# Experts of a mixture layer: the tokens of two pairs gathered at once in float32r halves, 22 weight tiles in flight, and a passage in four pieces

## The chip, the core and the metric

The kernel runs on one core of a Trainium2 chip. The metric is device time in microseconds (us) of one execution; the median of three runs stands for the kernel. Engines are named as in the profile: PE (TensorE, matrix products), DVE (VectorE), ACT (ScalarE), POOL (GpSimd) and SP (SyncE, which here issues the weight transfers).

## What is computed

Two transformer blocks over 256 tokens of width 1024, in float32. Block one is a retention branch and a convolution branch, merged, and then a mixture of 32 experts. Block two is a gated mixer and a dilated attention. The change lies in the experts and in the passage from the first block to the second:

```
def _hier_moe(u, p):
    ...
    top_w, top_i = lax.top_k(jax.nn.softmax(in_grp, axis=-1), EXPERT_TOP_K)   # 2 experts of a group
    ...
    for e in range(N_EXPERTS):                                                # 32 experts, 512 wide
        h = jax.nn.silu(t @ p['w_exp_gate'][e]) * (t @ p['w_exp_up'][e])
        y = y + combine[:, e:e + 1] * (h @ p['w_exp_down'][e])
...
h_lat = _layernorm(ALPHA * h_lat + gt_f * moe, p['ln2_g'], p['ln2_b'])
```

Every token goes to two experts; the reference runs all tokens through all experts with weights that are zero elsewhere. The kernel gathers up to 64 tokens for each expert and leaves the rest to a second pass behind a branch, which these inputs don't enter.

## The kernel before

**Experts.** Two experts form a pair, and a loop runs over 16 pairs. An object of the class `Pair` carries a pair through its steps. `gather` (L928) multiplies the normed tokens hn, 256 x 1024, by a selection matrix gt of 0 and 1 (256 tokens by 2 x 64 places) and so brings the tokens of the two experts to columns, eight chunks of 128x128 with two products each, float32; ACT (L932) and DVE (L934) take them out of PSUM by turns, with scale and shift, to xg. `products` (L945) makes gate and up in two halves, the 64 tokens of an expert as stationary columns, two experts side by side. `act` (L964, L965) makes silu(gate) * up, `turn` (L970) transposes it, ACT copies the result to hT (L972), `down` (L984) multiplies it by the second weight. `combine` (L991 to L999) splits the result of the pair before into two float32r halves and sends the rows back to their tokens by products with gT; `weights` (L956 to L960) prepares the gate weights. The order in the loop is written by hand with `after(...)`, which holds an instruction behind a named other one: the first half of the next pair's gather stands behind the up products, the second behind `turn`.

**Weights.** A pair takes 12 tiles of 128x2048, 1 MB each: gate, up, gate, up and down, two tiles for each of the halves. `moe_tiles` asks for them in order and `fetch` (L124) issues them on SP; each transfer stands behind the one before it on that queue. They go to slots in turn: five of the pool `ring`, some of the pools `ring3` (RING3), `x` (NX) and of the tag x8 (NX8), and further free spaces, 23 in rotation and one for the first tile. A slot is written anew when PE has done with its tile. With SP in order, one late slot holds all later transfers.

**Passage.** With the last `combine` done, DVE makes statistics (L1076, L1117), POOL raises the variance to the power -1/2 (L162; there is a branch ahead of it, which reads `cnti`: L1088), and DVE norms the two row blocks in one instruction each (L1123, 128x1024). PE transposes chunks of the normed rows (L1153), DVE and ACT make scaled features of them (L1161, L1162: ft, xl), and the first products of the mixer follow (L185 to L187). These products run in three parts: `split` makes of a float32 weight the float32r halves h_w (ACT, L179) and l_w (DVE, or POOL where `idle` is set, L181), and PE adds xh*h_w, xl*h_w and xh*l_w. The l_w of the first mixer tile are POOL's, held behind the power: `after(pows[0] if idle else ...)`. After the first quarter of the mixer's columns the residual gets its gain and shift (L1254, L1255), one row block on POOL, one on DVE.

In names of the rows below, `acc` is the memory of the residual rows, `cat` holds the identity for transposes, `mm`, `po`, `tr`, `sc`, `y` are PSUM tiles.

## Time and profile before

| | us |
|---|---|
| median of three runs (1492.33 to 1494.02) | 1493.73 |
| the profiled execution, its own time | 1494.24 |
| its span on the core | 1492.5 |
| PE busy in the span | 1437.1 (96%) |
| DVE busy | 931.9 (62%) |
| ACT busy | 557.2 (37%) |
| POOL busy | 125.1 (8%) |

Times in rows count from the start of the span. Outside the span 1.7 us of the execution lie. PE works nearly all the time over the whole span, so the totals say little; each stage has to be read by itself. The experts run from 500 to 961 us, the passage from there to about 1006 us, the mixer and the attention to the end. In a row of the timeline the first number is the start, the second the time from there to the end of the last instruction in the row, then engine, line, operation, result and operands; in brackets stands how long the engine stood before it and what ended that.

### The profile page before, as it was taken

How to read it: one execution, taken by the hardware profiler on the slowest of the kernel's cores; microseconds unless marked ns; L12 is line 12 of the kernel's file. 1: busy time of each engine (PE TensorE's matmuls, PEld its weight loads, DVE VectorE, ACT ScalarE, POOL GpSimd, SP SyncE). 2: the span in 40 equal slices, each digit the busy share in tenths (PEclk: the TensorE clock that was granted, in tenths of full speed). 3: DMA queues.
4: the chain of work that ended last, by engine and by line, in shares of the span. 5: the costliest groups of instructions: out<-in, count | busy, mean ns of one | idle time of the engine just before them, and what ended most of it. 6: DMA issues, size and time to landing. Idle time of an engine off the chain costs nothing. (4 is left out here: it accounts for less than half of the span.)

```text
span 1492.5 us, 23025 instructions
## 1 busy us (share of the span) xinstructions
PE 1437.1 (96%) x9391; PEld 1098.6 (74%) x9391; DVE 931.9 (62%) x1631; ACT 557.2 (37%) x834; POOL 125.1 (8%) x104
## 2 busy tenths in 40 slices
PE   7999999999999999999999999879999899999997
PEld 4888888888999544444444444369998799999995
DVE  3899998979656533333333333386668566676766
ACT  3855345332564211111111111154444545454543
POOL 0024021200000000000000000030000111101010
PEclk8999999999999999999999999999999999999999
DMA  8863454546777899999999999356554455655530
GB/s 345 339 216 113 155 211 157 197 156 226 288 292 305 317 373 419 420 420 419 420 420 420 420 420 419 151 202 249 183 199 162 149 209 167 209 174 194 184 114 29
DMA packets 60942, 390.37 MB, mean 262 GB/s; under 512 B 7840, under 2 KB 10400, under 8 KB 16800
## 3 DMA queue, kind: packets, MB, share of 16 engines
q1 hardware_dynamic: 55584, 378.37, 64.9%
q10 hardware_dynamic: 5248, 10.49, 2.9%
q8 instruction: 75, 1.23, 0.3%
q14 instruction: 35, 0.29, 0.1%
HBM read 377.29 MB, written 1.05 MB: 253 GB/s over the span
## 5 line engine op out<-in xcount | busy, mean ns | idle before, releaser
L181 DVE TENSOR_TENSOR l_w<-w,h_w 128x1024 fp32r<-128x1024 f32 x228 | 295.7, 1305 | 74.2 <-ACT h_w L179 70.3
L179 ACT CAST h_w<-w 128x1024 fp32r<-128x1024 f32 x232 | 239.4, 1048 | 263.9 <-PE mm L186 145.5
L185 PE MATMUL mm<-xh,h_w 128*128 128x256 f32 x704 | 201.4, 286 | 0.0
L187 PE MATMUL mm<-xh,l_w 128*128 128x256 f32 x704 | 199.4, 283 | 1.4 <-DVE l_w L181 1.4
L186 PE MATMUL mm<-xl,h_w 128*128 128x256 f32 x704 | 199.4, 283 | 0.0
L187 PEld LDWEIGHTS mm<-xh,l_w 128*128 128x128 f32 x704 | 135.3, 192 | 1.6 <-DVE l_w L181 1.6
L185 PEld LDWEIGHTS mm<-xh,h_w 128*128 128x128 f32 x704 | 135.3, 192 | 0.9
L186 PEld LDWEIGHTS mm<-xl,h_w 128*128 128x128 f32 x704 | 135.3, 192 | 0.1
L999 DVE TENSOR_TENSOR acc<-acc,sc 128x512 f32<-128x512 f32 x64 | 41.1, 684 | 135.6 <-PE sc L998 135.6
L185 PE MATMUL mm<-uh,h_w 128*128 128x256 f32 (+1 forms) x400 | 123.4, 309 | 0.8 <-ACT h_w L179 0.8
L187 PE MATMUL mm<-uh,l_w 128*128 128x256 f32 (+1 forms) x400 | 121.4, 304 | 2.7 <-DVE l_w L181 2.7
L945 PE MATMUL gate<-w,xg 128*64 128x512 f32 x512 | 121.9, 596 | 0.5
L186 PE MATMUL mm<-ul,h_w 128*128 128x256 f32 (+1 forms) x400 | 121.0, 303 | 0.0
L945 PE MATMUL up<-w,xg 128*64 128x512 f32 x512 | 120.0, 595 | 0.0
L331 DVE SCALAR_TENSOR_TENSOR cacc<-zp,pka,cacc 128x256 f32<-128x256 f32 x240 | 118.0, 511 | 1.7
L984 PE MATMUL y<-w,hT 128*64 128x512 f32 x512 | 113.9, 596 | 0.7 <-ACT hT L972 0.7
L945 PEld LDWEIGHTS up<-w,xg 128*64 128x64 f32 x512 | 40.4, 137 | 64.9 <-issue 63.9
L945 PEld LDWEIGHTS gate<-w,xg 128*64 128x64 f32 x512 | 40.2, 137 | 64.2 <-issue 62.4
L984 PEld LDWEIGHTS y<-w,hT 128*64 128x64 f32 x512 | 38.8, 136 | 63.8 <-issue 60.5
L187 PE MATMUL mm<-h_w,xl 128*128 128x256 f32 (+1 forms) x256 | 79.9, 313 | 2.7 <-DVE xl L1162 2.7
L187 PEld LDWEIGHTS mm<-uh,l_w 128*128 128x128 f32 x400 | 76.9, 193 | 7.1 <-DVE l_w L181 3.8
L185 PEld LDWEIGHTS mm<-uh,h_w 128*128 128x128 f32 x400 | 77.1, 193 | 6.7 <-ACT h_w L179 1.9
(411 smaller groups left out, 2848.2 us busy)
## 6 DMA issues: line engine op xcount, KB each, us to landing
w<-in_W_dram SPq DMA_DIRECT2D x343, 1024.0 KB, 10.6
sw<-raw ACTq DMA_DIRECT2D x48, 128.0 KB, 4.4
w<-in_W_dram SPq DMA_DIRECT2D x8, 512.0 KB, 11.4
xt<-in_xc_dram SPq DMA_DIRECT2D x4, 512.0 KB, 5.8
sw<-qk ACTq DMA_DIRECT2D x8, 256.0 KB, 4.2
v<-vt ACTq DMA_DIRECT2D x16, 128.0 KB, 2.4
cbt<-in_cb_dram SPq DMA_DIRECT2D x1, 1152.0 KB, 11.3
ya<-in_W_dram SPq DMA_DIRECT2D x2, 512.0 KB, 10.0
```

The lines of the kernel that those rows point to most:

```text
L179: high[:] = [A.copy(h, src)]
L181: low[:] = [(G if idle else V).tensor_tensor(l, src, h.bitcast(F32), op=OP.subtract)]
L185: T.matmul(ps, sh, mh, start=start, stop=False)
L186: T.matmul(ps, sh, ml, start=False, stop=False)
L187: return T.matmul(ps, sl, mh, start=False, stop=stop)
L331: V.scalar_tensor_tensor(cacc[:, m, :], src, pv("dw", m * 31 + t), cacc[:, m, :], op0=OP.mult, op1=OP.add)
L945: done = T.matmul(self.pgu[u][64 * j:64 * j + 64, :], self.xg[:, c, 64 * j:64 * j + 64], self.w[u][j][:, k * 512:(k + 1) * 512], start=c = ...
L984: T.matmul(self.py[n][64 * j:64 * j + 64, :], self.hT[:, c, 64 * j:64 * j + 64], w[j][:, o:o + 512], start=c == 0, stop=c == 3, tile_posit ...
L999: adds.append(V.tensor_tensor(acc[0][:, b, ns], acc[0][:, b, ns], pc, op=OP.add))
```

## The change

Gathers: pairs 0 and 1 are gathered as before. At pair 0 `halve` makes two float32r halves of hn, hh (ACT copies) and hl (DVE subtracts into a float32 tile `rest`, which takes one turn of a weight slot with tag x8, and ACT casts that into hl, which lies in the memory of hn itself). From then on each odd pair up to 13 gathers the two pairs that follow: `Gathering.chunks` makes 32 products of 128x256 (hh and hl, each by the selection of four experts) where two times 32 of 128x128 stood. Even pairs from 2 on don't gather; the second half of `combine` and `weights` moves behind their up products. Slots: NX8 goes from 6 to 5 and RING3 from 3 to 2, so 21 turn and 22 tiles are in flight; tag h gets a fourth buffer. Passage: the norm comes in four pieces of 512 columns, both row blocks of the left half first; POOL's l_w no longer wait for the power, and the other l_w of that stage wait for the last piece; both row blocks of gain and shift go to DVE, behind the last chunk of features. In block two's attention, arguments of `split` shift by one place: POOL now makes the l_w of the second half of the first weight and of the first half of the second, and the casts of the second weight wait for `fed`.

```diff
@@ -29,5 +29,5 @@
 NEG = -1e30
-RING, RING3 = 5, 3
+RING, RING3 = 5, 2
 NX = 3
-NX8 = 6
+NX8 = 5
@@ -179,3 +179,3 @@
             high[:] = [A.copy(h, src)]
-        with after(pows[0] if idle else hold.pop() if hold else la):
+        with after(None if idle else hold.pop() if hold else la):
             low[:] = [(G if idle else V).tensor_tensor(l, src, h.bitcast(F32), op=OP.subtract)]
@@ -903,2 +903,46 @@
+    def affine(dst, ps, m):
+        if m % 2:
+            A.activation(dst, ps, AF.Identity, scale=fA[:, m:m + 1], bias=fB[:, m:m + 1])
+        else:
+            low[:] = [V.tensor_scalar(dst, ps, fA[:, m:m + 1], fB[:, m:m + 1], op0=OP.mult, op1=OP.add)]
+    hnp = []
+    def halve():
+        hh = m2.tile([128, 2, 1024], F32R, name="hh", bufs=1)
+        rest = m1.tile([128, 2, 1024], F32, name="w", tag="x8", bufs=NX8)
+        for b in range(2):
+            A.copy(hh[:, b, :], hn[:, b, :])
+            V.tensor_tensor(rest[:, b, :], hn[:, b, :], hh[:, b, :].bitcast(F32), op=OP.subtract)
+        hl = m1.tile([128, 2, 1024], F32R, name="hl", tag="gb")
+        for b in range(2):
+            A.copy(hl[:, b, :], rest[:, b, :])
+        hnp[:] = [hh, hl]
+    class Gathering:
+        def __init__(self, *pairs):
+            n = 128 * len(pairs)
+            self.gt = m2.tile([128, 2, 256], F32R, name="gt", bufs=1)[:, :, 0:n]
+            self.xg = m2.tile([128, 8, 256], F32, name="xg", bufs=1)[:, :, 0:n]
+            for i, p in enumerate(pairs):
+                p.choose(self.gt, 1, 128 * i)
+                p.xg = self.xg[:, :, 128 * i:128 * i + 128]
+        def chunks(self, m0, name):
+            pg = ps2.tile([128, 2, 256], F32, name=name, bufs=2)[:, :, 0:self.gt.shape[2]]
+            for k in range(2):
+                m = m0 + k
+                for b in range(2):
+                    for i in range(2):
+                        done = T.matmul(pg[:, k, :], hnp[i][:, b, m * 128:(m + 1) * 128], self.gt[:, b, :],
+                                        start=b + i == 0, stop=b + i == 2)
+            for k in range(2):
+                affine(self.xg[:, m0 + k, :], pg[:, k, :], m0 + k)
+            return done
     class Pair:
@@ -906,8 +950,6 @@
-        def __init__(self, load, e0):
-            self.load, self.e0 = load, e0
-            self.gt = m2.tile([128, 2, 128], F32, name="gt", bufs=1)
-            self.choose(self.gt, 1)
+        def __init__(self, load, e0, xg=None):
+            self.load, self.e0, self.xg = load, e0, xg
-        def choose(self, t, k):
+        def choose(self, t, k, o=0):
             for b in range(2):
@@ -915,3 +957,4 @@
                     e = self.e0 + j
-                    low[:] = [V.tensor_scalar(t[:, b, 64 * j:64 * j + 64], iota, prw[:, 0, b, e:e + 1],
+                    at = o + 64 * j
+                    low[:] = [V.tensor_scalar(t[:, b, at:at + 64], iota, prw[:, 0, b, e:e + 1],
                                               prw[:, k, b, e:e + 1], op0=OP.is_equal, op1=OP.mult)]
@@ -919,5 +962,7 @@
         def gather(self, i, cuts=1):
             if i == 0:
-                self.xg = m2.tile([128, 8, 128], F32, name="xg", bufs=1)
-            xg = self.xg
+                self.gt = m2.tile([128, 2, 256], F32, name="gt", bufs=1)[:, :, 0:128]
+                self.choose(self.gt, 1)
+                self.xg = m2.tile([128, 8, 256], F32, name="xg", bufs=1)[:, :, 0:128]
             pg = [ps2.tile([128, 4 // cuts, 128], F32, name="tr", bufs=2) for _ in range(cuts)]
@@ -929,8 +974,3 @@
             for k in range(4):
-                m = 4 * i + k
-                if k % 2:
-                    A.activation(xg[:, m, :], pg[k], AF.Identity, scale=fA[:, m:m + 1], bias=fB[:, m:m + 1])
-                else:
-                    low[:] = [V.tensor_scalar(xg[:, m, :], pg[k], fA[:, m:m + 1], fB[:, m:m + 1], op0=OP.mult,
-                                              op1=OP.add)]
+                affine(self.xg[:, 4 * i + k, :], pg[k], 4 * i + k)
@@ -962,3 +1002,3 @@
         def act(self):
-            self.h = m2.tile([128, 512], F32, name="h", tag="h", bufs=3)
+            self.h = m2.tile([128, 512], F32, name="h", tag="h", bufs=4)
             A.activation(self.h, self.pgu[0], AF.Silu)
@@ -970,3 +1010,3 @@
                 done = T.transpose(ph[:, k, :], self.h[:, k * 128:(k + 1) * 128], ident)
-            self.hT = m2.tile([128, 4, 128], F32, name="hT", tag="h", bufs=3)
+            self.hT = m2.tile([128, 4, 128], F32, name="hT", tag="h", bufs=4)
             A.copy(self.hT, ph)
@@ -991,3 +1031,3 @@
             V.tensor_tensor(py, py, gtf[:, ns], op=OP.mult)
-            yh, yl = (m2.tile([128, 512], F32R, name=k, tag="h", bufs=3) for k in ("ysh", "ysl"))
+            yh, yl = (m2.tile([128, 512], F32R, name=k, tag="h", bufs=4) for k in ("ysh", "ysl"))
             A.activation(yh, py, AF.Copy, scale=self.ws)
@@ -1017,5 +1057,9 @@
-    last_pair, pair = None, Pair(lambda k: tiles[k], 0)
-    for p in range(16):
+    def nth(p):
+        return Pair(lambda k, o=12 * p: tiles[o + k], 2 * p)
+    pairs = [nth(p) for p in range(16)]
+    for p, pair in enumerate(pairs):
         moe_tiles(12 * p + 12)
+        before = pairs[p - 1] if p else None
         if p == 0:
@@ -1034,22 +1078,36 @@
             with after(done):
-                last_pair.combine(0)
+                before.combine(0)
         done = pair.products(1, 0)
-        if last_pair:
+        late_sum = p and p % 2 == 0
+        if p == 0:
+            start()
+        elif not late_sum:
             with after(done):
-                last_pair.combine(1)
+                before.combine(1)
                 pair.weights()
-        else:
-            start()
         done = pair.products(1, 1)
         pair.act()
-        if p < 15:
-            next_pair = Pair(lambda k, o=12 * p + 12: tiles[o + k], 2 * p + 2)
-            with after(done):
-                next_pair.gather(0)
-            done = pair.turn()
-            with after(done):
-                next_pair.gather(1)
-        else:
-            pair.turn()
-        pair.down()
+        with after(done):
+            if p == 0:
+                pairs[1].gather(0)
+                done = pair.turn()
+                pairs[1].gather(1)
+                halve()
+            elif late_sum:
+                before.combine(1)
+                done = pair.turn()
+                pair.weights()
+            elif p < 15:
+                g = Gathering(*pairs[p + 1:p + 3])
+                g.chunks(0, "sc")
+                done = g.chunks(2, "sc")
+                with after(done):
+                    done = pair.turn()
+                with after(done):
+                    g.chunks(4, "tr")
+                    done = g.chunks(6, "sc")
+            else:
+                done = pair.turn()
+        with after(done):
+            pair.down()
         if p == 15:
@@ -1057,3 +1115,2 @@
                 pair.combine(n)
-        last_pair, pair = pair, next_pair
@@ -1097,4 +1154,5 @@
                 pair = Pair(load, 0)
-                for i in range(2):
-                    pair.gather(i)
+                g = Gathering(pair)
+                for m in range(0, 8, 2):
+                    g.chunks(m, "tr")
                 pair.weights()
@@ -1120,5 +1178,6 @@
     bridge(KN["BR"][1], st.rearrange("p a b -> p (a b)"), mv.rearrange("p a b -> p (a b)"), rs)
-    for b in range(2):
-        r = acc[0][:, b, :]
-        V.tensor_scalar(r, r, mv[:, b, 0:1], rs[:, b:b + 1], op0=OP.subtract, op1=OP.mult)
+    for n in range(2):
+        for b in range(2):
+            r = acc[0][:, b, n * 512:(n + 1) * 512]
+            normed = V.tensor_scalar(r, r, mv[:, b, 0:1], rs[:, b:b + 1], op0=OP.subtract, op1=OP.mult)
     p2.close()
@@ -1242,3 +1301,3 @@
             for q in range(2):
-                wh, wl = split(w[:, q * 1024:(q + 1) * 1024], idle=nb == half == 0, ha=lead if 4 * nb + 2 * half + q >= 3 else None)
+                wh, wl = split(w[:, q * 1024:(q + 1) * 1024], idle=nb == half == 0, ha=lead if 4 * nb + 2 * half + q >= 3 else None, la=normed)
                 for cq in range(2):
@@ -1247,3 +1306,3 @@
                     if nb == 0 and 0 < c < 5:
-                        chunk(c + 3, done)
+                        fed = chunk(c + 3, done)
                     for b in range(2):
@@ -1252,5 +1311,6 @@
         if nb == 0:
-            for b, E in enumerate((G, V)):
-                E.tensor_tensor(xs[:, b, :], xs[:, b, :], g2, op=OP.mult)
-                E.tensor_tensor(xs[:, b, :], xs[:, b, :], b2, op=OP.add)
+            for b in range(2):
+                with after(fed):
+                    V.tensor_tensor(xs[:, b, :], xs[:, b, :], g2, op=OP.mult)
+                    V.tensor_tensor(xs[:, b, :], xs[:, b, :], b2, op=OP.add)
             rt, rf, _, along, _ = rms_scales(m3, ps3, 4)
@@ -1351,3 +1411,3 @@
                 first = qd == g == 0
-                wh, wl = split(w[:, a * 1024:(a + 1) * 1024], first and i == 0, square if first and i + a == 1 else None,
+                wh, wl = split(w[:, a * 1024:(a + 1) * 1024], square if first and i + a == 1 else None,
                                fed if first and i == 1 else None)
```

In the rows of orders, a name ahead of the arrow is what an instruction writes; "waits DVE_49" is a semaphore of DVE, DMAHW the transfer lanes. On PE, between the up products of an odd pair and its down products, before:

```order
L945 MATMUL up<-w,xg 64x512 x8
L928 MATMUL tr<-gt,hn 128x128 x8
L970 MATMUL tr<-cat,h 128x128 x4
L945 MATMUL gate<-w,xg 64x512
L928 MATMUL tr<-gt,hn 128x128 x8
L984 MATMUL y_5321<-w,hT 64x512 x4
L984 MATMUL y_5322<-w,hT 64x512 x4
```

and after (of the alternating products of hh and hl one pair stands for four in each place):

```order
L985 MATMUL up<-w,xg 64x512 x8
L942 MATMUL sc<-gt,hh 128x256
L942 MATMUL sc<-gt,hl 128x256
...
L1010 MATMUL tr<-cat,h 128x128 x4
L942 MATMUL tr<-gt,hh 128x256
L942 MATMUL tr<-gt,hl 128x256
...
L1024 MATMUL y_5956<-w,hT 64x512 x4
L1024 MATMUL y_5957<-w,hT 64x512 x4
```

The gather stays on both sides of the transposes, with half the instructions for twice the experts, into two kinds of PSUM tile; the product of the next pair that stood ahead of the second half is gone from there. The next place is pair 0 and what follows it on ACT and on SP. Before, ACT's evictions of pair 1's gather behind hT, and SP's transfers of the same time (L124 with one PE wait each):

```order
L972 COPY hT<-tr 128x512 [waits PE_49]
L932 ACTIVATE xg<-tr,fv_3734,fv_3733 128x128 [waits DVE_49,Activation_49]
L932 ACTIVATE xg<-tr,fv_3734,fv_3733 128x128 [waits DVE_49] x3
L993 ACTIVATE ysh<-y_5187,ws 128x512 [waits DVE_49]
...
L124 DMA w<-in_W_dram 128x2048 [waits DMAHW2_49,PE_49]
L124 DMA w<-in_W_dram 128x2048 [waits DMAHW3_49,PE_49]
```

and after, with the transfer of tile 26 (tiles count from 0) on SP as the line that waits for DVE and ACT:

```order
L1012 COPY hT<-tr 128x512 [waits PE_49]
L906 ACTIVATE xg<-tr,fv_3734,fv_3733 128x128 [waits DVE_49,Activation_49]
L906 ACTIVATE xg<-tr,fv_3734,fv_3733 128x128 [waits DVE_49]
L921 CAST hl<-w 128x1024 [waits PE_49]
L906 ACTIVATE xg<-tr,fv_3734,fv_3733 128x128 [waits DVE_49]
L921 CAST hl<-w 128x1024
L906 ACTIVATE xg<-tr,fv_3734,fv_3733 128x128 [waits DVE_49]
...
L124 DMA w<-in_W_dram 128x2048 [waits DMAHW0_49,PE_49]
L1145 TENSOR_LOAD cnti [waits DVE_49]
L1145 ISA x2
L124 DMA w<-in_W_dram 128x2048 [waits DMAHW1_49,DVE_49,Activation_49]
L124 DMA w<-in_W_dram 128x2048 [waits DMAHW2_49,PE_49]
```

Two casts have come between the evictions, the first of which waits for PE, and one transfer waits for ACT instead of PE. The third place is the passage on POOL, before:

```order
L1088 TENSOR_LOAD cnti [waits DVE_49]
L1089 COMPARE_AND_BRANCH
...
L162 TENSOR_TENSOR rstd<-var_e,mhalf 128x2 [waits DVE_49,Pool_49]
L181 TENSOR_TENSOR l_w<-w,h_w 128x1024 [waits DMAHW4_49,DMAHW5_49,DMAHW3_49,DMAHW6_49,DMAHW0_49,DMAHW7_49,PE_49,Activation_49]
L1254 TENSOR_TENSOR acc<-acc,w 128x1024 [waits DMAHW7_49,DVE_49,PE_49]
L1255 TENSOR_TENSOR acc<-acc,w 128x1024 [waits DMAHW0_49,Pool_49]
```

and after:

```order
L877 CAST prw<-rbf 128x64 [waits DVE_49,PE_49,Activation_49]
L181 TENSOR_TENSOR l_w<-w,h_w 128x1024 [waits DMAHW4_49,DMAHW5_49,DMAHW2_49,DMAHW7_49,PE_49,Activation_49]
L1145 TENSOR_LOAD cnti [waits DVE_49]
L1146 COMPARE_AND_BRANCH
...
L162 TENSOR_TENSOR rstd<-var_e,mhalf 128x2 [waits DVE_49,Pool_49]
L1233 TENSOR_TENSOR rt<-rt,mhalf 128x2 [waits DMAHW5_49,DMAHW4_49,DMAHW7_49,DMAHW2_49,DVE_49]
```

The two l_w (the second of them stands here) moved from behind the power to ahead of the branch, and the gain and shift left POOL.

## Rows read from the trace of the kernel before

**Rows 1.** Stretches: us, busy of PE, PEld, DVE, ACT, POOL, clock, DMA share, GB/s.
```profile
500.00:510.00 10.00, 10.00 (x54) 4.51 (x53) 6.57 (x27) 3.50 (x10) 0.00 (x0) 1.00 0.51 173
...
520.00:530.00 10.00, 9.89 (x60) 5.82 (x62) 3.13 (x9) 2.32 (x5) 0.00 (x0) 1.00 0.61 234
...
740.00:920.00 180.00, 175.95 (x888) 83.90 (x886) 62.62 (x143) 26.36 (x49) 0.00 (x0) 1.00 1.01 420
...
940.00:945.00 5.00, 5.00 (x24) 2.08 (x22) 1.88 (x3) 0.00 (x0) 0.00 (x0) 1.00 0.96 398
945.00:950.00 5.00, 5.00 (x24) 2.01 (x22) 2.02 (x5) 0.60 (x1) 0.00 (x0) 1.00 0.28 116
```

**Rows 2.** Timeline of PE, pair 6: start, us, row, idle before.
```profile
676.92 3.65 PE L945 MATMUL gate<-w,xg 128*64 128x512 f32 x16
...
696.73 2.05 PE L928 MATMUL tr<-gt,hn 128*128 128x128 f32 x16 [0.68 <-ACT hT L972]
698.71 7.14 PE L984 MATMUL y<-w,hT 128*64 128x512 f32 x32
705.63 1.08 PE L945 MATMUL gate<-w,xg 128*64 128x512 f32 x4
```

**Rows 3.** Who L945 waited for: us, times.
```profile
  DMA w<-in_W_dram: 1.6, 6
```

**Rows 4.** Timeline of PE in the mixer.
```profile
1059.72 0.28 PE L186 MATMUL mm<-xl,h_w 128*128 128x256 f32 x1
1059.84 0.28 PE L187 MATMUL mm<-xh,l_w 128*128 128x256 f32 x1
```

**Rows 5.** Groups by line and form, PE, 497 to 962 us: busy, mean ns, idle before.
```profile
L928 PE MATMUL tr<-gt,hn 128*128 128x128 f32 x512 | 65.6, 281 | 8.0 <-ACT hT L972 7.4 <-DVE gt L916 0.5
```

**Rows 6.** Timeline of ACT at pair 0.
```profile
500.26 0.46 ACT L932 ACTIVATE xg<-tr,fv,fv 128x128 f32<-128x128 f32 x1 [3.48 <-DVE xg L934]
...
526.99 0.46 ACT L932 ACTIVATE xg<-tr,fv,fv 128x128 f32<-128x128 f32 x1 [0.53 <-DVE xg L934]
```

**Rows 7.** The page: a group of ACT, and DMA issues (count, size, us to landing).
```profile
L179 ACT CAST h_w<-w 128x1024 fp32r<-128x1024 f32 x232 | 239.4, 1048 | 263.9 <-PE mm L186 145.5
...
w<-in_W_dram SPq DMA_DIRECT2D x343, 1024.0 KB, 10.6
```

**Rows 8.** Timeline of PE, end of the experts and both passages.
```profile
959.45 1.94 PE L984 MATMUL y<-w,hT 128*64 128x512 f32 x8
...
973.22 0.33 PE L1153 MATMUL mm<-cat,acc 128*128 128x128 f32 x1 [2.26 <-DVE acc L1123]
975.97 0.47 PE L1153 MATMUL mm<-cat,acc 128*128 128x128 f32 x1 [2.42 <-DVE acc L1123]
...
992.15 0.50 PE L187 MATMUL mm<-h_w,xl 128*128 128x512 f32 x1 [2.72 <-DVE xl L1162]
...
1177.22 0.47 PE L1153 MATMUL mm<-cat,acc 128*128 128x128 f32 x1 [3.98 <-DVE acc L1220]
```

**Rows 9.** Timeline of DVE in the passage.
```profile
970.35 5.56 DVE L1123 TENSOR_SCALAR acc<-acc,mv,rstd 128x1024 f32<-128x1024 f32 x2 [0.88 <-POOL rstd L162]
975.83 1.21 DVE L181 TENSOR_TENSOR l_w<-w,h_w 128x1024 fp32r<-128x1024 f32 x1
...
985.02 3.43 DVE L1254 TENSOR_TENSOR acc<-acc,w 128x1024 f32<-128x1024 f32 x1
...
988.83 2.93 DVE L1255 TENSOR_TENSOR acc<-acc,w 128x1024 f32<-128x1024 f32 x1
```

**Rows 10.** Timeline of POOL in the passage.
```profile
970.28 5.08 POOL L181 TENSOR_TENSOR l_w<-w,h_w 128x1024 fp32r<-128x1024 f32 x2
984.84 2.53 POOL L1254 TENSOR_TENSOR acc<-acc,w 128x1024 f32<-128x1024 f32 x1 [9.47 <-PE po L1153]
```

**Rows 11.** Another norm of 128x1024 (L693): duration ns min, median, max.
```profile
L693 DVE TENSOR_SCALAR cz<-cz,mv,rstd x2: 812/813/814, 401.7 to 408.3; 128x1024 f32<-128x1024 f32 x2
```

**Rows 12.** Stretch in the passage, columns as in rows 1.
```profile
975.80:979.00 3.20, 3.03 (x11) 2.74 (x12) 3.17 (x7) 2.52 (x5) 0.00 (x0) 0.50 0.78 264
```

## The prediction

> **What bounds the kernel now.** I read the stretch table first. From 740 to 920 us TensorE (PE) works 176 of 180 us, and the transfers run at 420 GB/s with a DMA share of 1.01 all the while [rows 1]; the stretch from 560 reads alike: two resources are full at once, and the question is which has slack. The reader should see PE's period: pair 6 begins at 676.92 and pair 7 at 705.63, 28.71 us a pair [rows 2]. The queue needs longer: a tile is 1,048,576 B, at 420 GB/s 2.497 us, twelve of them 29.96 us. PE is faster than its supply and lives on a lead: weights loaded before the experts began. It has not run out at the end. Behind the last expert tile the queue still brings two rows and four tiles of block two, 5.24 MB; from 940 to 950 it moves (398 + 116) x 5 = 2.57 MB [rows 1], and the other 2.67 MB take 6.4 us at 420, so the last expert tile landed near 934, say 935.5 with the time until it is signalled. The last down products end at 961.39 [rows 8]. Half of a down group of 7.14 us [rows 2] needs that tile, so it was wanted near 957.8: a lead of some 22 us is left. Over the whole kernel PE waited 1.6 us for weights in the gate and up products [rows 3]. So PE bounds this stage with 22 us in hand, and a saving above that belongs to the queue.
>
> Behind the experts a chain of short steps bounds: PE stands 2.26 and 2.42 us before the first transposes of the normed rows and 2.72 us at 992.15 [rows 8]; that is the passage to block two.
>
> **Gathers.** Removed: in seven of eight two-pair periods (pairs 2 to 15), 64 products L928, 16 records in 2.05 us, 1.98 from the first start to that of the next group [rows 2], 0.112 us each by the way they follow each other: 7.2 us. Added: 32 products 128x256 in fp32r; such products follow each other at 0.12 us in the mixer [rows 4], 3.84 us. The stall of 0.68 us ahead of the second gather half [rows 2], 7.4 us over the stage [rows 5], goes too: both halves no longer need the buffer that the ACT copy hT frees, and in even pairs the combine stands there. Two pairs go from 57.4 to 57.4 - 3.3 - 1.3 = 52.8, or 52.4 with both stalls and the small waits at a pair's turn gone. Over seven periods PE alone would gain 32 to 35 us and end the experts near 928. That is **before the last weight has landed even now** (935.5). The exact price of the new products therefore drops out of the sum.
>
> **Queue.** What counts is when the last expert tile lands. Before, the queue has a hole: from 500 to 510 it moves 173 GB/s and from 520 to 530 234 [rows 1], while PE frees the first slots; from some 530 on it is full. Two slots fewer push two tiles, 5.0 us, out of the early stock, and since the queue is full from there to the end, the last tile is 5.0 us later: 940.5. The second step is `halve`. Its `rest` lies in one of the five slots that rotate with tag x8, and the row of SP's order shown above says which transfer that is: tile 26 waits for DVE and ACT, that is for the second `hl` cast, and all later tiles stand behind it on SP. `hl` shares the buffer of hn and so waits for the last gather of pair 1. Before, that gather's last eviction on ACT starts at 526.99 [rows 6], and the one before it 1 us earlier; in the changed order a cast stands before each. With the casts at 1.05 us (the mean of L179 [rows 7]) the second ends near 528.2 if nothing else moves. Pair 0 also carries the two subtractions of `halve` on DVE, 1.2 us each by the like subtraction at 975.83 [rows 9], ahead of an eviction; I take 1 us for them, bounds 0 and 2.4. The hh copies go into ACT's idle 3.48 us before 500.26 [rows 6] and cost nothing; without that gap they would cost 2.1 us. So tile 26 is issued near 529.2. It lands not sooner than its own 2.5 us later, and not later than the 10.6 us that a tile takes with a full queue [rows 7]; as the queue is nearly empty then, I take 4.5: 533.7. Behind it are 165 tiles x 2.497 = 412 us: the last lands at 945.7, and with half a down group of 3.6 us the experts end near **949.3 instead of 961.4: -12 us**. The bounds: -17 (the slot of `rest` costs nothing, 940.5 + 3.6), and -7 (full queue latency at tile 26). In the last six or seven pairs PE is then starved, some 20 us in waits of up to 1.6 us (a gate group takes 3.65 us [rows 2], its two tiles 5.0).
>
> The fourth buffer of tag h, the later combine of even pairs and the wider evictions (four of 256 columns on DVE and on ACT per two pairs for sixteen of 128) lie beside 28 us of PE work a pair with DVE busy a third of it [rows 1]: nothing in the sum. If that cover failed, a late xg would cost under 1 us a pair, and the queue's slack takes it up.
>
> **Passage.** Before, DVE's two norm operations take 5.56 us while POOL makes the two l_w of the first av tile in 5.08 us, from the same moment [rows 9, 10]. The same operation on another tile takes 0.81 us [rows 11]: each norm ended just behind a POOL operation. So DVE was held, PE got its first block after 2.26 us and the second after 2.42, and its clock stood at 0.50 (1.2 GHz) from 975.8 to 979.0 [rows 8, 12]. The same again at L1254: 3.43 us on DVE beside 2.53 us on POOL [rows 9, 10], and PE stands 2.72 us. The Trainium skill, "SBUF — State Buffer", section "SBUF: two separate sides", has the shared port pair of DVE and GpSimd as an exclusive lock, held for a whole instruction by whichever starts first; by it the norm alone would take what [rows 11] show, and the trace agrees. After: POOL's l_w no longer wait for the power and stand ahead of the branch; the av tile lands about 1.4 us behind the end of the down products (945.7 + 2.5 for the rows + 2.5), the casts follow, and POOL works from +2.6 to +7.3 us after it, while the power was done at +8.9 (just before 970.35 [rows 9]) and began 0.7 us sooner. The norm comes in four pieces, some 0.45 us each. PE could win 2.26 + 2.42 - 0.5 = 4.2, half of the 3.2 us at the low clock, the 2.72, and 1.6 more if the clock falls behind that gap as well: 10.1 us at most. DVE, busy without a hole in between, wins less: 5.56 - 1.8 = 3.8 in the norm, and of 3.43 + 2.93 us at L1254 and L1255 [rows 9] it gets four operations of 1.2: 1.5 us; 5.3 in all, 4.5 if two pieces are held. I take **-7**, between the two, and keep -4.5 and -9. POOL's margin is about 1 us: if it is late, the power is late behind it.
>
> **Second passage.** PE stands 3.98 us at 1177.22 [rows 8], behind a DVE operation held like those. The changed split gives POOL the l_w of the second half of the first weight and of the first half of the second, instead of both of the first, and DVE more of its own: the overlap moves but does not go. **-0.5**, bounds -1.5 and +1 (one l_w of 1.2 us more on DVE).
>
> **Sum.** The profiled execution took 1494.24 us, 0.5 above the median of 1493.73: no correction. 1494.24 - 12 - 7 - 0.5 = **1474.7, say 1474.5 us**.
>
> **The rivals.** *The weights keep up* and PE's whole saving arrives: 1494.24 - 33 - 7.5 = 1453.7. It would need twelve tiles in 26.2 us, 480 GB/s, and no stretch of the experts shows over 420 for long: 0.03. *The slot of `rest` costs nothing*, only the two slots do: 1494.24 - 17 - 7.5 = 1469.7. For it speaks that SP's other waits at that place are on PE and are met by then; against it the row of the order: 0.13. *The passage gives nothing back*, since POOL's l_w come late and the power stands behind them, or DVE is held elsewhere: 1494.24 - 12 = 1482: 0.11. *Slower: the clock falls in the starved pairs.* Behind each gap of 2.3 to 2.7 us in the passage the clock went to 0.50 [rows 8, 12], while the stage with its stalls of 0.68 us in each pair went on at 1.00 [rows 1, 2]. Waits of 1.6 us lie between. At half the clock a gate group takes some 7 us where the queue gives its two tiles in 5.0, so PE is the bound, and a pair takes 52 us, not 30: +22 us for each pair at the low level. One such pair already turns -19.5 into +2.5, 1497; two give 1519. Once PE is the slow one it no longer waits, which speaks for a return to 1.00: 0.05.
>
> **How the numbers follow.** My forecast has 0.68, the rivals 0.03, 0.13, 0.11 and 0.05. The range runs from the two good bounds together (-17, -9 and -1.5 give 1466.7), 1466, to just past the failed passage, 1483; outside lie the first rival, the slower one and the far tails of the bounds. Faster by over 0.2% (3 us, about what a measurement of this kernel can tell from none): 0.93; within it 0.02; slower 0.05.
>
> **What would show it.** Right: transfers at 420 GB/s without a hole from about 534 to about 950; waits of gate, up and down on weight transfers of some 20 us in all, none above 2 us, from pair 9 or so; no L928 stall; the clock at 1.00 throughout; POOL's l_w ended before the power, norm pieces under 0.6 us, no half-clock stretch in the passage. Wrong: tile 26 issued well before or after 529; experts that end before 940 or after 955; a clock of 0.50 among the experts; a norm piece above 1 us, or PE standing over 2 us before the first transposes.

## The result, and the profile after

The changed kernel takes 1472.93 us (median of four runs, 1472.26 to 1475.58); the kernel before, run beside it, 1493.12 us. The ratio is 0.9868, 95% interval 0.9853 to 0.9883: 20.2 us less, 1.3%. The forecast was 1474.5 us, range 1466 to 1483.

The profiled execution took 1473.43 us, its span 1471.7 us. Set against the profile of before, by stages, in us:

| | before | after | difference | forecast |
|---|---|---|---|---|
| first gate product of pair 0, from the span's start | 500.38 | 496.63 | -3.75 | 0 |
| from there to the last landing of an expert tile | 435.2 | 446.4 | +11.2 | +10.1 |
| from the first gate product to the end of the last down product | 461.0 | 450.0 | -11.0 | -12 |
| from there to PE's last product | 523.7 | 517.5 | -6.1 | -7.5 |

The first row is no work of the change. In the first 40 us the profile of before has PE's clock at 0.83, that of after at 1.00, with the same products; and in the twelve kernels of the experiments the first gate product stands between 496.6 and 502.6, at 498.0 in one with the old experts. It is a spread from one execution to the next, and stages are compared from here on by their own beginnings. The ends of the down products are those of [rows 8] (959.45 + 1.94) and of this row of after:

```profile
938.87 7.80 PE L1024 MATMUL y<-w,hT 128*64 128x512 f32 x32 [0.68 <-ACT hT L1012]
```

The stretches of after that answer to [rows 1] (columns as there):

```profile
500.00:510.00 10.00, 10.00 (x53) 4.53 (x50) 9.42 (x27) 2.20 (x3) 0.00 (x0) 1.00 0.52 196
...
520.00:530.00 10.00, 10.00 (x56) 4.46 (x57) 4.63 (x14) 3.87 (x7) 0.00 (x0) 1.00 0.48 182
...
740.00:920.00 180.00, 168.13 (x760) 77.11 (x758) 56.13 (x119) 21.52 (x36) 0.00 (x0) 1.00 1.01 420
...
940.00:945.00 5.00, 5.00 (x24) 2.54 (x22) 0.00 (x0) 0.00 (x0) 0.00 (x0) 1.00 1.03 419
945.00:950.00 5.00, 3.49 (x13) 1.24 (x9) 3.88 (x6) 3.24 (x4) 0.79 (x1) 1.00 0.95 395
```

In the third row the queue moves 420 GB/s as before, and PE, which worked 176 of 180 us, works 168: it has become the one that waits. The clock stays at 1.00. In the last two the transfers go on past the last down product (946.67); before they had ended by then.

What PE waited for from 500 to 955 us (total us, times, longest):

```profile
PE up L985 <- DMA w<-in_W_dram: 8.0, 9, 1.3
PE gate L985 <- DMA w<-in_W_dram: 3.8, 4, 1.1
PE y L1024 <- ACT hT L1012: 3.4, 7, 0.7
```

These are waits of the products alone, and such a view counts only from the end of the product before. The weight loads (PEld), which come ahead of the products, stood longer (total us, times, longest):

```profile
PEld up L985 <- DMA w<-in_W_dram: 17.2, 11, 2.2
PEld gate L985 <- DMA w<-in_W_dram: 7.5, 5, 2.0
```

Together they are 24.7 us; the 1.6 us of [rows 3] are weight loads too. The stall of [rows 5] has gone from 7.4 us ahead of the gathers to 3.4 us ahead of the down products, since in even pairs little now stands between the transposes and these. PE, from pair 7's gather for pairs 8 and 9 to pair 9 (timeline as in [rows 2]):

```profile
704.24 0.60 PE L1010 MATMUL tr<-cat,h 128*128 128x128 f32 x4
...
705.61 0.28 PE L942 MATMUL sc<-gt,hh 128*128 128x256 f32 x1
705.73 0.28 PE L942 MATMUL sc<-gt,hl 128*128 128x256 f32 x1
...
706.64 7.14 PE L1024 MATMUL y<-w,hT 128*64 128x512 f32 x32
...
731.04 7.14 PE L1024 MATMUL y<-w,hT 128*64 128x512 f32 x32 [0.46 <-ACT hT L1012]
...
741.39 4.74 PE L985 MATMUL up<-w,xg 128*64 128x512 f32 x16
...
748.62 3.65 PE L985 MATMUL gate<-w,xg 128*64 128x512 f32 x14 [0.36 <-DMA w<-in_W_dram]
```

The gather products follow each other at 0.12 us, as those of [rows 4], and two down groups stand 24.40 us apart. At 741.39 an up group takes 4.74 us where it took 3.65: the lead has run out at pair 9, and from there the pairs go at the queue's pace, 59 to 60 us by twos (twice 29.96), where the PE-bound ones before them took 52.4.

The late slot, on ACT at pair 0 (answers to [rows 6]), and on SP:

```profile
521.81 1.04 ACT L921 CAST hl<-w 128x1024 fp32r<-128x1024 f32 x1 [1.25 <-PE tr L973]
522.76 0.45 ACT L906 ACTIVATE xg<-tr,fv,fv 128x128 f32<-128x128 f32 x1
523.12 1.03 ACT L921 CAST hl<-w 128x1024 fp32r<-128x1024 f32 x1
524.05 0.46 ACT L906 ACTIVATE xg<-tr,fv,fv 128x128 f32<-128x128 f32 x1
```

```profile
524.17 0.33 SPq L124 DMA_DIRECT2D w<-in_W_dram  x1
```

```profile
SPq L124 <- ACT xg L906: 11.6, 1, 11.6
```

The second cast ends at 524.15, tile 26 is issued at 524.17, and SP had stood there for 11.6 us (the third view, waits of SP's queue; it names the eviction that ran as the wait ended).

The passage after, on PE, DVE and POOL (answers to [rows 8 to 10]):

```profile
955.99 0.59 PE L1140 MATMUL up<-gtf,bst 128*24 128x256 f32 x2 [2.41 <-PEq L1146]
...
957.38 0.44 PE L1212 MATMUL mm<-cat,acc 128*128 128x128 f32 x2
...
958.47 0.50 PE L185 MATMUL mm<-h_w,xh 128*128 128x512 f32 x1
```

```profile
955.58 1.92 DVE L1182 TENSOR_SCALAR acc<-acc,mv,rstd 128x512 f32<-128x512 f32 x4 [0.88 <-POOL rstd L162]
...
969.87 2.35 DVE L1314 TENSOR_TENSOR acc<-acc,w 128x1024 f32<-128x1024 f32 x2
972.14 2.35 DVE L1315 TENSOR_TENSOR acc<-acc,w 128x1024 f32<-128x1024 f32 x2
```

```profile
949.21 4.70 POOL L181 TENSOR_TENSOR l_w<-w,h_w 128x1024 fp32r<-128x1024 f32 x2 [455.47 <-ACT h_w L179]
954.84 0.70 POOL L162 TENSOR_TENSOR rstd<-var_e,mhalf 128x2 f32<-128x2 f32 x1 [0.93 <-DVE var_e L160]
```

POOL's l_w run from 2.54 to 7.24 us behind the end of the down products, the power from 8.17; the norm takes 1.92 us for 5.56, gain and shift 4.62 us for both row blocks on DVE alone. PE's first mixer product stands 11.8 us behind the down products, not 16.0 as in this row of before:

```profile
977.37 0.77 PE L185 MATMUL mm<-h_w,xh 128*128 128x512 f32 x1
```

The gaps of 2.26, 2.42 and 2.72 us are gone; in their place PE stands 2.41 us at the branch (L1146), for which POOL, busy with l_w until 953.91, now comes late. No half-clock stretch follows here: the clock is 1.00 from 955 to 1000 us. The gap is not free even so: the left half of the norm is done at 956.58, but the filling products that PE makes behind the branch (L1140) last until 957.4, so the transposes start some 0.8 us late.

### The profile page after: what moved, and what is told of

It is laid out like the page before. It is cut to its first block, busy times and chain, and to the rows that moved or that the text cites. A ratio compares the mean times of both kernels' runs of the same rounds, so it can differ in the third digit from the quotient of the medians.

```text
span 1471.7 us, 22523 instructions
## 1 busy us (share of the span) xinstructions
PE 1412.4 (96%) x9167; PEld 1081.7 (73%) x9167; DVE 916.7 (62%) x1609; ACT 551.4 (37%) x810; POOL 118.1 (8%) x102
## 5 line engine op out<-in xcount | busy, mean ns | idle before, releaser
L985 PE MATMUL up<-w,xg 128*64 128x512 f32 x512 | 128.2, 596 | 8.1 <-DMA w<-in_W_dram 8.0
L985 PE MATMUL gate<-w,xg 128*64 128x512 f32 x512 | 125.7, 596 | 3.9 <-DMA w<-in_W_dram 3.8
L985 PEld LDWEIGHTS gate<-w,xg 128*64 128x64 f32 x512 | 45.6, 137 | 66.8 <-issue 53.3
L1024 PEld LDWEIGHTS y<-w,hT 128*64 128x64 f32 x512 | 44.8, 136 | 63.5 <-issue 54.3
L185 PE MATMUL mm<-h_w,xh 128*128 128x256 f32 (+1 forms) x256 | 80.7, 315 | 0.0
## 6 DMA issues: line engine op xcount, KB each, us to landing
cbt<-in_cb_dram SPq DMA_DIRECT2D x1, 1152.0 KB, 11.6
```

Source lines behind the costliest of these rows:

```text
L185: T.matmul(ps, sh, mh, start=start, stop=False)
L985: done = T.matmul(self.pgu[u][64 * j:64 * j + 64, :], self.xg[:, c, 64 * j:64 * j + 64], self.w[u][j][:, k * 512:(k + 1) * 512], start=c = ...
L1024: T.matmul(self.py[n][64 * j:64 * j + 64, :], self.hT[:, c, 64 * j:64 * j + 64], w[j][:, o:o + 512], start=c == 0, stop=c == 3, tile_posit ...
```

## The experiments

Times of whole runs scatter: the 14 of the kernel before on one chip lie between 1489.2 and 1500.07 us, 0.7%. So ratios are to the kernel before on the same chip, and stages are read from profiles, one for each kernel. All kernels together (us; "landed" is the last expert tile and "experts" the end of the last down product, both from the first gate product; "rest" from there to PE's last product):

| kernel | median | ratio, 95% interval | landed | experts | rest |
|---|---|---|---|---|---|
| before | | 1 | 435.2 | 461.0 | 523.7 |
| changed | 1472.93 | 0.9868 [0.9853, 0.9883] | 446.4 | 450.0 | 517.5 |
| changed, again | 1475.27 | 0.9869 [0.9852, 0.9885] | 446.5 | 450.1 | 516.6 |
| before, 22 slots | 1495.72 | 1.0002 [0.9982, 1.0022] | 440.2 | 461.2 | 524.2 |
| low half left out of the products | 1478.84 | 0.9895 [0.9859, 0.9931] | 446.5 | 450.2 | 514.9 |
| no rest, no hl | 1471.86 | 0.9834 [0.9793, 0.9875] | 440.3 | 444.0 | 518.4 |
| halves earlier | 1469.8 | 0.9826 [0.9783, 0.9869] | 439.1 | 442.8 | 520.4 |
| half the weights | 1450.35 (one run) | | | 423.9 | 516.6 |
| old passage | 1487.43 | 0.9951 [0.9934, 0.9967] | 446.4 | 450.1 | 524.7 |
| POOL's l_w held again | 1482.1 (one run) | | 446.5 | 450.2 | 524.5 |
| norm in two pieces | 1472.96 (one run) | | 446.4 | 450.1 | 517.1 |
| gain and shift on POOL again | 1485.39 (one run) | | 446.4 | 450.1 | 523.7 |
| old split in the attention | 1476.01 | 0.9878 [0.9856, 0.9901] | 446.4 | 450.1 | 520.5 |
| halves earlier, two edits more | 1466.12 | 0.9801 [0.9785, 0.9816] | 439.1 | 442.8 | 516.7 |

The theory: with the cheaper gathers the weight queue, not PE, sets the end of the experts; the end is the last landing plus half a down group, and the last landing is set by the two slots and by the slot lent to `rest`; behind the experts the gain comes from POOL not running beside DVE. The main rival: PE's products set the end, and the slots are hidden.

**The changed kernel again.**

> The changed kernel once more, as the base for the other kernels of this call. Both theories: 450 us from the first gate product to the last down product, within 0.5 us, whatever the moment at which the experts start; the rest behind it 515 to 520 us, with the third wait for the shifted rows of the rotation between 10 and 13 us; 20 us under the kernel before.

The experts took 450.1 us, the rest 516.6, the time was 19.9 us under before. As expected.

**22 slots alone, in the kernel before.**

```diff
-RING, RING3 = 5, 3
+RING, RING3 = 5, 2
-NX8 = 6
+NX8 = 5
```

> The kernel before with one change alone: 22 weight tiles in flight instead of 24, all else as it was. Queue theory: the last expert tile lands 5 us later (about 440 us after the first gate product, 435 in the kernel before), the lead of 22 us shrinks to about 17 and PE does not starve, so the experts still take 461 us and the time is that of the kernel before, 1493 us within 0.2%. Rival (two slots fewer cost time by themselves): 1498 us, with the experts 5 us longer.

The last tile lands 5.0 us later, exactly two tiles of the queue, and the experts take 461.2 us. What PE waited for in that stage, the two longest sums of the view (total us, times, longest), has no weight transfer in it:

```profile
PE tr L928 <- ACT hT L972: 7.4, 11, 0.7
PE tr L970 <- DVE h L965: 0.9, 1, 0.9
```

The lead was slack, as the prediction read it, and two slots fewer cost nothing as long as PE is the slow one.

**The low half left out of the gather products.**

```diff
-                    for i in range(2):
-                        done = T.matmul(pg[:, k, :], hnp[i][:, b, m * 128:(m + 1) * 128], self.gt[:, b, :],
-                                        start=b + i == 0, stop=b + i == 2)
+                    done = T.matmul(pg[:, k, :], hnp[0][:, b, m * 128:(m + 1) * 128], self.gt[:, b, :],
+                                    start=b == 0, stop=b == 1)
```

> The changed kernel with the gather products of the low half left out: 16 products for two pairs instead of 32 (the rest and hl are still made, and the slot is lent). PE has 1.9 us less in each of seven double gathers, 13 us in all. Queue theory: the end of the experts does not move, PE waits some 13 us more for weights, and the time is 1473 us within 2 us. Rival (PE's products set the end): 1460 us.

PE lost 12 us of work (two pairs, while PE is the bound, take 50.6 us and not 52.4, seven times) and the experts took 450.2 us: nothing. What left the products came back as waits of the weight loads (view of PEld, 500 to 953 us):

```profile
PEld up L984 <- DMA w<-in_W_dram: 23.5, 12, 2.2
PEld gate L984 <- DMA w<-in_W_dram: 13.8, 8, 2.1
```

37.3 us on weights where the changed kernel has 24.7. That is the rival's end: PE's products do not set the end of the experts. (The time of the whole run, 17 us under before, agrees within the intervals.)

**No rest and no low half.**

```diff
-        rest = m1.tile([128, 2, 1024], F32, name="w", tag="x8", bufs=NX8)
         for b in range(2):
             A.copy(hh[:, b, :], hn[:, b, :])
-            V.tensor_tensor(rest[:, b, :], hn[:, b, :], hh[:, b, :].bitcast(F32), op=OP.subtract)
-        hl = m1.tile([128, 2, 1024], F32R, name="hl", tag="gb")
-        for b in range(2):
-            A.copy(hl[:, b, :], rest[:, b, :])
-        hnp[:] = [hh, hl]
+        hnp[:] = [hh, hh]
```

> The changed kernel without the second half of hn: neither the rest nor hl is made, no weight slot is lent, and the gather products run over hh twice, so PE has the same products; the values gathered are twice the first half. Queue theory: tile 26 waits for PE alone and is issued about 10 us sooner; the last expert tile lands 5 to 6 us earlier counted from the first gate product, and the time is 1467 to 1468 us. Rival (the late slot is hidden): 1473 us within 2 us.

**The halves earlier.**

```diff
-        late_sum = p and p % 2 == 0
+        late_sum = p % 2 == 1 and p < 15
         if p == 0:
             start()
+            halve()
...
-            if p == 0:
-                pairs[1].gather(0)
-                done = pair.turn()
-                pairs[1].gather(1)
-                halve()
-            elif late_sum:
+            if late_sum:
```

> The changed kernel with hn halved earlier: the halves are made behind the start of the residual, pairs 1 and 2 are gathered together at pair 0, pairs 3 and 4 at pair 2, and so on, pair 15 alone at pair 14. So the slot of the rest comes free before pair 1 is gathered. Queue theory: no transfer stands behind the late cast; the last expert tile lands 5 to 6 us earlier, counted from the first gate product (446 us in the changed kernel, 440 to 441 here), the experts take 444 to 445 us, not 450, and the time is 1467 to 1468 us. Rival (PE's own work sets the end, the late slot is hidden): the time of the changed kernel, 1473 us within 2 us, since PE has as many products.

In both, the same number of gather products for a double gather and no late slot: the last tile lands at 440.3 and 439.1 us, the experts take 444.0 and 442.8. In the second the casts of hl end 12.4 us behind the first gate product (498.26 there), not 27.5: 15 us sooner (timeline of ACT, that kernel):

```profile
508.34 1.04 ACT L921 CAST hl<-w 128x1024 fp32r<-128x1024 f32 x1 [0.75 <-DVE w L918]
...
509.64 1.03 ACT L921 CAST hl<-w 128x1024 fp32r<-128x1024 f32 x1
```

So the lent slot costs 6 to 7 us of the queue's time, and 440 is what 22 slots cost alone. The second of these kernels computes what the changed one does. By the medians it is some 6 us faster, less than the 7 us of the experts, since its rest took 3 us longer (below); the intervals of the two ratios overlap.

**Half the weights.**

```diff
         while len(tiles) < n:
+            if len(tiles) >= 24 and len(tiles) % 2:
+                tiles.append(tiles[-1])
+                continue
```

> The changed kernel with half of the weight transfers left out from tile 24 on: each tile is loaded once and stands for its neighbour too, so the queue needs 15 us a pair; the values are those of the wrong weights. Queue theory: PE never waits for weights, the pairs take 52.4 us by twos, and the experts end 424 to 428 us after the first gate product instead of 450: 22 to 26 us less, as the prediction had it for PE alone. Rival (PE's waits are not from the weights, or the new gathers cost more than 0.12 us a product): 440 us or more.

PE alone, with the queue out of the way: 423.9 us, 37.1 under before, and 27.93 + 24.34 = 52.3 us for two pairs, from down group to down group. The stretches (columns as in [rows 1]) show PE without a gap beside a queue that has gone to 165 GB/s:

```profile
560.00:740.00 180.00, 180.00 (x865) 82.68 (x863) 64.39 (x141) 23.93 (x40) 0.00 (x0) 1.00 0.78 302
740.00:900.00 160.00, 160.00 (x773) 74.64 (x771) 57.21 (x121) 22.18 (x37) 0.00 (x0) 1.00 0.46 165
```

The change saves PE 37 us in the experts, and the queue takes 26 of them back (450.0 - 423.9).

**The old passage.**

```diff
-        with after(None if idle else hold.pop() if hold else la):
+        with after(pows[0] if idle else hold.pop() if hold else la):
...
-    for n in range(2):
-        for b in range(2):
-            r = acc[0][:, b, n * 512:(n + 1) * 512]
-            normed = V.tensor_scalar(r, r, mv[:, b, 0:1], rs[:, b:b + 1], op0=OP.subtract, op1=OP.mult)
+    for b in range(2):
+        r = acc[0][:, b, :]
+        V.tensor_scalar(r, r, mv[:, b, 0:1], rs[:, b:b + 1], op0=OP.subtract, op1=OP.mult)
...
-            for b in range(2):
-                with after(fed):
-                    V.tensor_tensor(xs[:, b, :], xs[:, b, :], g2, op=OP.mult)
-                    V.tensor_tensor(xs[:, b, :], xs[:, b, :], b2, op=OP.add)
+            for b, E in enumerate((G, V)):
+                E.tensor_tensor(xs[:, b, :], xs[:, b, :], g2, op=OP.mult)
+                E.tensor_tensor(xs[:, b, :], xs[:, b, :], b2, op=OP.add)
```

> The changed kernel with the old passage to block two: the norm in two pieces, POOL's l_w behind the power, gain and shift on POOL and DVE. If the passage is worth what the mixer's start shows (PE 9 to 10 us earlier at the end of the first quarter of the mixer, counted from the last down product), this kernel is 7 to 10 us slower than the changed one, its first mixer product stands 16 us behind the last down product and not 12. Rival (the attention gives most of it back, since its round trips through memory and not PE set its pace): 2 to 4 us slower only.

(The kernel also drops `la=normed` and `fed`, which belong to these hunks.) The rest took 8.1 us longer than in the changed kernel run beside it, 7.1 longer than in its first profile, and PE is 7.7 us later in the mixer. The medians stand 12.2 us apart; the profiled execution, 1481.43 us, was the fastest of its four by 5.4. The first theory holds: the passage is worth 7 to 8 us in the profiles, up to 12 by the medians. Its three parts apart ("later in the mixer" is counted from the last down product to the products of the mixer's second quarter, against the first profile of the changed kernel):

**POOL's l_w held again** (the first of the three hunks alone).

> The changed kernel with POOL's two l_w of the first mixer tile held behind the power again, so that they run beside the norm; all else as changed. If POOL holds DVE, the four norm pieces take 4 us or more, not 1.9, the first mixer product stands 14 to 16 us behind the last down product and not 12, and the end of the mixer's first quarter is 3 to 5 us later. Rival (the pieces are short enough to slip between): under 1 us.

PE is 6.0 us later in the mixer. DVE and POOL in that kernel:

```profile
957.25 5.95 DVE L1182 TENSOR_SCALAR acc<-acc,mv,rstd 128x512 f32<-128x512 f32 x4 [0.88 <-POOL rstd L162]
```

```profile
957.17 4.83 POOL L181 TENSOR_TENSOR l_w<-w,h_w 128x1024 fp32r<-128x1024 f32 x2
```

The four pieces that take 1.92 us beside an idle POOL take 5.95 beside two POOL operations of 4.83, more than the two whole operations of [rows 9]. The first two pieces end at 959.80 and 962.28, each 0.28 us behind the end of a POOL operation (959.52 and 962.00); the other two, with POOL idle, take 0.54 each. Small pieces do not slip between. The rule cited in the prediction (the Trainium skill, "SBUF — State Buffer", section "SBUF: two separate sides": an exclusive lock on the shared port pair, held for the whole instruction) agrees with the two that waited for POOL's end.

**The norm in two pieces** (the second hunk alone, with `normed` kept for the l_w).

> The changed kernel with the norm in two instructions of 1024 columns and not in four of 512; POOL's l_w early as in the changed kernel. If the earlier l_w are what freed DVE, the two take 1.6 us together, and the mixer starts within 0.7 us of the changed kernel. Rival (the cut into pieces gives the gain): the mixer starts 2 us later or more.

```profile
955.58 1.53 DVE L1181 TENSOR_SCALAR acc<-acc,mv,rstd 128x1024 f32<-128x1024 f32 x2 [0.88 <-POOL rstd L162]
```

1.53 us for the two, and the first mixer product 12.1 us behind the down products, against 11.8 and 12.0 in the two profiles of the changed kernel. In the mixer PE is 0.2 us behind the first profile of the changed kernel and level with the second. The cut into four pieces, which gave this part of the change its name, is worth nothing that shows; what the norm gains comes from POOL's l_w being out of its way.

**Gain and shift on POOL again** (the third hunk alone).

> The changed kernel with gain and shift of the residual as before, one row block on POOL, one on DVE, not behind the last chunk of features. If POOL holds DVE, DVE's two operations take some 6 us for 2.4, PE stands 2 us or more behind a late xl, and the end of the mixer's first quarter is 3 to 4.5 us later. Rival: within 1 us.

PE is 7.7 us later in the mixer, more than expected. PE stands behind DVE held by POOL, and the clock falls to 0.50:

```profile
973.77 2.98 DVE L1313 TENSOR_TENSOR acc<-acc,w 128x1024 f32<-128x1024 f32 x1
```

```profile
972.87 2.79 POOL L1313 TENSOR_TENSOR acc<-acc,w 128x1024 f32<-128x1024 f32 x1 [11.52 <-PE po L1212]
```

```profile
979.28 0.80 PE L187 MATMUL mm<-h_w,xl 128*128 128x512 f32 x1 [3.17 <-DVE xl L1221]
```

Some 1.4 us of the 7.7 stand there before gain and shift begin: behind the gap at the branch this execution has a half clock, which the changed kernel's has not. The two single prices, 6.0 and 6.3 without it, come to more than the 7.7 of the whole old passage: the parts hide each other in part.

**The old split in the attention.**

```diff
-                wh, wl = split(w[:, a * 1024:(a + 1) * 1024], square if first and i + a == 1 else None,
+                wh, wl = split(w[:, a * 1024:(a + 1) * 1024], first and i == 0, square if first and i + a == 1 else None,
                                fed if first and i == 1 else None)
```

> The changed kernel with the split of the first attention weights as before: POOL makes both l_w of the first weight, the casts of the second weight don't wait for the features. By the prediction the new split is worth 0.5 us: so +0.5 us here (-1 to +1.5), with PE standing some 4 us instead of 2.9 us before the first transposes of the attention. Rival: the 3.5 us that the changed kernel gives back in the attention come from the new split; then this kernel is 3 us faster than the changed one.

1.4 us later at the first transposes of the attention, 2.2 us some 8 us on; no gain at the later place where the changed kernel gives back (3.7 us of waiting there, for 3.0). The new split is worth 1.4 to 2 us at its place, and the give-back is not its doing. In the medians only 0.7 us of it show, which is within the scatter.

**The give-back.** Counted from the last down product, PE in the changed kernel is 10 us ahead at the first transposes of the attention and 6.2 us at the first scores (1224.67). In between stands the third round trip of the rotation: `raw` goes out on ACT's queue (L1425) and comes back with its rows shifted; then DVE multiplies raw, POOL multiplies sw, and a l_w behind these on DVE is held by POOL (DVE, POOL, PE of the changed kernel):

```profile
1215.78 1.23 DVE L1427 TENSOR_TENSOR raw<-raw,cct 128x1024 f32<-128x1024 f32 x1 [6.58 <-DMA sw<-raw]
1216.92 3.37 DVE L181 TENSOR_TENSOR l_w<-w,h_w 128x1024 fp32r<-128x1024 f32 x1
```

```profile
1215.82 3.40 POOL L1426 TENSOR_TENSOR sw<-sw,cct 128x1024 f32<-128x1024 f32 x1 [17.13 <-DMA sw<-raw]
```

```profile
1220.34 0.39 PE L187 MATMUL mm<-xh,l_w 128*128 128x256 f32 x1 [3.00 <-DVE l_w L181]
```

The wait follows the round trip one for one (from the first issue to DVE's product; PE's wait for l_w in us, over the kernels): 9.9 and 1.4 before, 10.2 and 1.7 with the low half left out, 10.5 and 2.0 with 22 slots, 11.3 and 2.8 without the rest, 11.5 and 3.0 changed, 11.8 and 3.3 with the old passage, 12.2 and 3.7 with the old split, 12.9 and 4.4 with earlier halves: always the trip less 8.5 us. In the changed kernel half a clock follows (0.50 from 1221.1 to 1224.5 us) and costs some 1.6 us more: the 22 products from 1220.34 take 4.3 us, where 0.12 us each would make 2.6. Why the trip is longer in most of the changed kernels is open: it shares the engines of the queue with the weights, and its four parts land up to 6 us apart, but no run takes one of them away.

**Both improved.** Earlier halves, three filling products per column ahead of the branch instead of two, and the rotation's products, with their sum as a function `rotate`, behind the next l_w:

```diff
-"BR": (2, 1)
+"BR": (3, 1)
...
+        if qd == 0 and g == 2:
+            late_turn.append(rotate)
+        else:
+            rotate()
...
+            while late_turn:
+                with after(low[0]):
+                    late_turn.pop()()
             A.copy(raw[:, 2 * i:2 * i + 2, :], ps)
             step()
```

> The kernel with hn halved earlier and two edits more: at the first attention quarter the two rotation products of the third group (one on POOL, one on DVE) stand behind the l_w of the next group's first weight, and the filling products ahead of the branch in the passage are three per column, not two. Theory: the experts take 443 us as with the earlier halves; PE does not stand 3 to 4.4 us at the third round trip of the shifted rows, and the clock stays at 1.00 there and in the passage, so the part behind the last down product takes 511 to 514 us; in all 4 to 6 us under the kernel with earlier halves, 29 to 31 us under the kernel before, ratio 0.980. Rival (the wait goes elsewhere: the scores then wait for the rotated rows): no more than 1 us under the kernel with earlier halves, ratio 0.9826.

The fastest kernel of the study, ratio 0.9801 [0.9785, 0.9816], 30 us under before. The whole time is what was expected, but the way to it is not: the rest took 516.7 us, not 511 to 514, 0.2 us more than in the changed kernel again. The long wait on l_w is gone, and smaller ones stand in its place (what PE waited for behind the experts):

```profile
PE s L1476 <- DVE qk L1429: 1.3, 1, 1.3
PE mm L186 <- DVE l_w L181: 0.8, 1, 0.8
...
PE mm L185 <- DVE zt L1463: 0.7, 1, 0.7
```

2 to 3 us ahead of the changed kernel at 1226 us of that profile, it is level again at 1290: the rival's mechanism for the attention. Against the kernel with earlier halves it is 1.2 us ahead at the first mixer product (that one had a half clock at the branch), level just ahead of the third round trip, 5.5 us ahead behind it and 3.7 us at the end. What the deferred rotation is worth by itself stays unclear.

## Why the prediction was right, step by step

- **The lead of 22 us, PE the bound before.** Right: 22 slots moved the last landing by 5.0 us and the time by nothing.
- **PE alone would gain 32 to 35 us, two pairs 52.4 to 52.8.** 37.1 us and 52.3: a little more, and, as said, out of the sum.
- **Queue.** The two slots: 5.0 us, measured alone at 5.0. Tile 26: forecast to be issued 28.8 us after the first gate product and to land at 33.3, measured 27.5 and 32.2; the subtractions on DVE cost less than the 1 us taken. The 165 tiles behind it took 414.1 us, not 412. The end came at 450.0 instead of 448.9. (The 10.6 us that the forecast took for a tile with a full queue are the median of all 343 transfers; from 900 to 915 us a tile of before lands 19.9 us behind its issue. Only a bound rested on it.) The -12 is -11.0, and the mechanism is the one forecast. The rival in which the slot of `rest` costs nothing fell with the 11.6 us wait of SP; the two kernels without it show that its price is 6 to 7 us, where the forecast had 5.
- **Waits of PE.** Forecast some 20 us, of up to 1.6; the weight loads waited 24.7 us, the longest 2.2, and 26 us lie between the changed kernel and PE alone. (The products' own waits, 11.8 us with 1.3 the longest, miss what passed while the product before still ran.) They begin at pair 9, as forecast. The slower rival, a half clock in the starved pairs, did not come: 1.00 throughout.
- **Passage, -7.** Mis-sized: PE is 9.0 us ahead in the mixer's second quarter, 10 by the attention, and its undoing costs 7 to 12. The step that failed is "DVE, busy without a hole in between, wins less": PE's gaps and the half clock behind them all went, so the 10.1 us counted on PE's side were the better estimate. And the cut into four pieces was priced (0.45 us each) as a part of it, though it has no share.
- **A new wait that the forecast left out**: 2.41 us of PE at the branch, since POOL's l_w stand ahead of its load of the branch's value. Most of it lies beside the wait for the power; some 0.8 us of it delays the transposes, and more is lost where the clock falls behind it.
- **Second passage, -0.5.** -1.1 at the place (a gap of 2.90 us for 3.98), 1.4 to 2.2 against the old split. What the forecast did not have at all is the attention's third round trip, which gives 2 to 4 us back. So -7.5 behind the experts came out at -6.1 in the profile (-8.7 to -3.2 in the six profiles whose kernels leave the rest as the changed one has it), from two errors of opposite sign.
- **The sum.** -11.0 and -6.1 make -17.1 in the profiles; the 3.75 us with which this execution began sooner make the rest of its 20.8. The medians say 20.2 and 19.9. The 2 to 3 us between 17.1 and these lie within the interval of the ratio (0.3%, 4.5 us wide) and the scatter of the rest from profile to profile. So the mechanism was right, but that the total came within 1.6 us of the forecast is in part luck: the stages alone give 2.4 us less than the forecast's 19.5.

## What to carry to other kernels

When two resources are both full, work out how long a lead the hidden one has before pricing a saving on the other: here 37 us saved on TensorE were worth 11, because the weight queue had 22 us in hand and the change itself spent half of that on slots. Slots taken from the ring of a saturated queue were paid in full at the end of the stage: two fewer moved the last landing by exactly two tiles. A slot that was only lent cost 6 to 7 us when it came back late and nothing when it came back 15 us sooner, so a loan has to be given back before the queue fills. And what freed VectorE beside GpSimd was that GpSimd's long operations moved to another time; cutting VectorE's own operation into four pieces did nothing.

## What was not expected of the hardware

- The same gap of PE ahead of the filling products at the branch (1.4 to 3.1 us in twelve profiles) is followed by half the clock in three of them (gaps of 2.41, 2.70 and 3.12 us) and by the full clock in nine, with gaps of 2.41 and 2.90 us among them; the length of the gap alone doesn't tell.
- One round trip through memory of the same four transfers takes from 9.9 to 12.9 us among kernels with the same instructions there, and PE's wait behind it follows to the tenth of a us.
- Executions with the same products up to there differ by up to 6 us at the first gate product. PE's clock in the first 40 us is 0.83 in one and 1.00 in another, but that does not order them (0.96 in one that gets there at 502.4): a change of that size in one stage must be counted from the stage's own beginning.
